# The low part of each freshly transposed y block is computed from PSUM instead of from its copy in SBUF

## The chip, the cores and the metric

The kernel runs on one core of a Trainium2 chip. The metric is the device time of one execution in microseconds (us). The time of a kernel is the median of its runs. One further execution was recorded by the hardware profiler; the durations of single instructions come from that one.

In the profile PE is the matrix engine and PEld its weight load, DVE is the vector engine, ACT the activation engine, POOL the general engine (GpSimd), and SP issues most DMAs. Each engine works through its own queue in order. L1266 is line 1266 of the kernel.

## The reference, cut to what matters

A decoder trunk of two layers runs over a prompt of 2048 tokens (width 1024) and, with the same weights, over eight sample tokens. Everything is float32. Each layer computes

```
u = RMSNorm(x) @ W_in                      # W_in: 1024 x 4880
y = [ mLSTM | Mamba-2 SSD | sliding-window attention ]   # 3 x 512 columns, each with its gate and norm
x = x + concat(y) @ W_out                  # W_out: 1536 x 1024
```

It also returns the state of each of the three mixers. The change touches only the way in which `concat(y)` is brought into `@ W_out`.

## The kernel before, in words

**Precision.** A float32 product is made of three products of a faster format (`F32R`). Each operand is split into a high part, which is the value rounded to that format, and a low part, the value less its high part. The product is then high x high + high x low + low x high.

**Tiling.** The prompt of each layer is cut into four blocks of 512 tokens, so there are eight block passes. A pass runs the input projection by groups of 512 columns, and every group runs over eight chunks of 128 rows of `W_in`. The output projection of a pass (`g == 'out'`) is placed between the groups of the next pass. It has two halves of 512 output columns, and each half runs over twelve chunks `k` of 128 rows of `W_out` (in the last pass the two halves take turns). A chunk is twelve matmuls of 128x128 by 128x512 in `multiply` (L519 with the activations as the moving operand or L521 the other way round): four output tiles, three products each.

**y blocks.** y is kept in SBUF tiles (`yA`, `yB`, `yC`, in the `quad` tiles). Chunks 0 to 3 (mLSTM) and 4 to 7 (SSD) hold tokens on the partitions and must be transposed; chunks 8 to 11 (attention) are already transposed. `prep_y` makes the operands of a chunk, one chunk ahead. When a chunk of k < 8 comes up for the first time (`new`), it

1. transposes the block with four PE instructions (L1252) into `pt`, one of the four PSUM banks of the ring `mx`;
2. lets ACT write the high part `yh` from `pt` (L1259), scaled by the norm weight;
3. lets ACT copy `pt` back over the block in SBUF, `blk` (L1263), where the second half of the projection will find it transposed;
4. puts `low` (L1266, on DVE) into a list of late work. It is emitted in `multiply`, after the second of the four tiles of the chunk before.

`low` computes `yl = blk * weight - yh`. In all there are 192 chunks of y, of which 64 are new (eight in each of the eight passes). For the other 128 there is no transpose and `pt` is `blk` itself.

**Order of the rest.** Mixers, gates and the sample tokens' work are generators ("streams"). `pump` is called after a tile of a chunk and takes a step of a stream if an accounting clock in the program (`Clock`) says that the engines are not too far behind and that the next `mx` bank will be free. The condition on the bank is this line:

```
if st[4] <= now and max(ck.t.values()) <= now + back and ck.free_at(self.rings['mx'][-4]) <= now:
```

`free_at` is the end, by that clock, of the last write or read of the tile that had the bank. The tile framework (`schedule_with_timeline_sim=True`) places semaphores between engines and may change the order further. During the first half of an output projection the streams are mostly the mLSTM of the next pass (`mix_a`, which asks for ten `mx` banks per 128 tokens), the end of the attention of the current pass (`main_c`) and the sample tokens' work.

Of the kernel before, what the change touches and what calls it, by code (L numbers as in the profile page):

```python
# [184 lines left out]
class Build:  # L185
# [1057 lines left out]
    def prep_y(self, ch):  # L1243

        nc, S, k = self.nc, ch['S'], ch['k']
        Y, L = [S['yA'], S['yB'], S['yC']][k // 4], S['L']
        blk = Y[:, :, (k % 4) * 128:(k % 4) * 128 + 128] if k < 8 else Y[:, k % 4, 0:512].rearrange("p (t c) -> p t c", c=128)
        new = ch['new']
        if new:
            pt = self.mx()  # L1250
            for t in range(4):
                nc.tensor.transpose(pt[:, t * 128:t * 128 + 128], blk[:, t, :], self.ident)  # L1252
            pt = pt.rearrange("p (t c) -> p t c", c=128)
        else:
            pt = blk
        i = k % 2

        yh, yl = (self.xTh[i], self.xTl[i]) if S['last'] else self.F[2 * i:2 * i + 2]
        nc.scalar.activation(yh.rearrange("p (t c) -> p t c", c=128), pt, AF.Copy, scale=L['ynw'][:, k:k + 1])  # L1259

        if new:

            nc.scalar.activation(blk, pt, AF.Copy)  # L1263

        def low():
            nc.vector.scalar_tensor_tensor(yl.rearrange("p (t c) -> p t c", c=128), blk, L['ynw'][:, k:k + 1],  # L1266
                                           yh.bitcast(F32).rearrange("p (t c) -> p t c", c=128),
                                           op0=ALU.mult, op1=ALU.subtract)

        self.late.append((0, low))  # L1270
        ch['y'] = (yh, yl)
# [664 lines left out]
```

## Time and profile before

| | |
|---|---|
| runs, us | 2997.62, 3002.35, 2995.71; median 2997.62 |
| profiled execution, us | 2994.12 |
| its span, first to last instruction, us | 2992.3 |
| PE busy | 2903.5 us, 97% of the span |
| DVE busy | 1912.3 us, 64% |
| ACT busy | 1235.0 us, 41% |
| POOL busy | 920.3 us, 31% |
| mean granted clock of PE | 0.991 |

The span leaves out 1.8 us of the profiled execution. A busy share is an average over the whole span. The chain is the work that ended last, followed back from the last instruction to whatever released each step.

### The profile page before, as it was taken

Reading aid. Unit: us, or ns where it says so; the run is one execution under the profiler, and the core shown is the slowest. Engines: PE = TensorE matmul, PEld = TensorE weight load, DVE = VectorE, ACT = ScalarE, POOL = GpSimd, SP = SyncE. Lnnn points to the kernel's source line nnn. Section 1 sums busy time; section 2 is a strip of 40 time slices with the busy share of each in tenths; the row PEclk is TensorE's granted clock in tenths of the full one; section 3 lists DMA queues with packets and bytes.
Section 4 is the critical chain, followed back from the end, with each engine's and each line's share of the span. In section 5 each row is a group of like instructions: output and inputs, shape, how many; then the busy total and the mean of one; then the engine's idle time right before and its main releaser. Section 6 shows DMA issues by size and latency. Waiting matters only on the chain.

```text
span 2992.3 us, 42253 instructions
## 1 busy us (share of the span) xinstructions
PE 2903.5 (97%) x14454; PEld 2373.4 (79%) x14454; DVE 1912.3 (64%) x4323; ACT 1235.0 (41%) x3219; POOL 920.3 (31%) x968
## 2 busy tenths in 40 slices
PE   8999999999999999999999999999999999999988
PEld 7787877788878888888788778887887778788876
DVE  6378567778476763477644686477755677645774
ACT  5343555235432453325544345432444225532344
POOL 5336325244131430116422552332421132200321
PEclk9999999999999999999999999999999999999999
DMA  8755558754575434655556745687545754355533
GB/s 279 241 197 168 174 184 284 248 170 141 164 247 189 151 117 143 199 171 182 184 187 215 240 159 183 205 274 232 161 156 177 244 174 160 131 163 165 177 112 124
DMA packets 245995, 558.82 MB, mean 187 GB/s; under 512 B 49308, under 2 KB 82236, under 8 KB 245732
## 3 DMA queue, kind: packets, MB, share of 16 engines
q1 hardware_dynamic: 245780, 556.12, 57.6%
q8 instruction: 114, 1.87, 0.3%
q14 instruction: 101, 0.83, 0.1%
HBM read 430.46 MB, written 127.87 MB: 187 GB/s over the span
## 4 chain that ended last, share of the span: by engine, by line
PE 71%; DVE 13%; DMA 8%; POOL 3%; ACT 2%; issue 2%; SPq 1%; POOLq 0%; DVEq 0%; ACTq 0%
PE pj L519 29%; PE pj L521 27%; DMA wr<-in_w_in 2%; PE mx L1203 2%; PE mx L1152 2%; PE mx L984 1%; DMA unit<-bcd 1%; DVE quad L659 1%; PE mx L542 1%; PE mx L541 1%; POOL hl L498 1%; ACT unit L1173 1%; PE mx L993 1%; PE mx L1252 1%; DMA unit<-us 1%
## 5 line engine op out<-in xcount | busy, mean ns | idle before, releaser
L521 PE MATMUL pj<-hl,xTh 128*128 128x512 f32 (+1 forms) x3072 | 945.4, 383 | 17.2 <-ACT hl L494 7.6
L519 PE MATMUL pj<-xTh,hl 128*128 128x512 f32 x2240 | 727.5, 402 | 4.8 <-ACT xTh L1259 2.9
L521 PEld LDWEIGHTS pj<-hl,xTh 128*128 128x128 f32 x3072 | 564.6, 189 | 129.0 <-DVE quad L562 8.3
L521 PE MATMUL pj<-hl,xTl 128*128 128x512 f32 (+1 forms) x1536 | 580.4, 381 | 0.0
L519 PE MATMUL pj<-parts,hl 128*128 128x512 f32 x2016 | 518.9, 404 | 15.1 <-DVE parts L1266 8.3
L519 PEld LDWEIGHTS pj<-xTh,hl 128*128 128x128 f32 x2240 | 421.5, 190 | 100.9 <-ACT xTh L1259 3.9
L519 PEld LDWEIGHTS pj<-parts,hl 128*128 128x128 f32 x2016 | 366.9, 189 | 96.1 <-DVE parts L1266 11.2
L519 PE MATMUL pj<-xTl,hl 128*128 128x512 f32 x1120 | 436.0, 398 | 1.9 <-DVE xTl L1266 1.9
L498 POOL TENSOR_TENSOR hl<-wr,hl 128x512 fp32r<-128x512 f32 (+1 forms) x232 | 318.9, 1380 | 356.3 <-ACT hl L494 311.2
L521 PEld LDWEIGHTS pj<-hl,xTl 128*128 128x128 f32 x1536 | 291.1, 189 | 52.5
L1195 POOL TENSOR_TENSOR parts<-parts,cst 128x512 fp32r<-128x512 f32 x120 | 158.6, 1339 | 409.0 <-ACT parts L1188 392.3
L519 PEld LDWEIGHTS pj<-xTl,hl 128*128 128x128 f32 x1120 | 211.2, 189 | 47.7 <-DVE xTl L1266 2.3
L1266 DVE SCALAR_TENSOR_TENSOR parts<-quad,lp,parts 128x512 fp32r<-128x512 f32 x168 | 143.0, 852 | 155.4 <-ACT quad L1263 62.4
L494 ACT ACTIVATE hl<-wr 128x512 fp32r<-128x512 f32 (+1 forms) x232 | 142.2, 615 | 234.2 <-PE mx L542 49.6
L1032 POOL TENSOR_TENSOR unit<-quad,rpqn 128x256 f32<-128x256 f32 x32 | 24.3, 759 | 441.6 <-PE mx L951 166.8
L1173 ACT ACTIVATE unit<-unit,c_m,c_sc 128x128 f32<-128x128 f32 x256 | 123.3, 483 | 69.3 <-DVE c_m L1164 68.8
L1259 ACT ACTIVATE parts<-quad,lp 128x512 fp32r<-128x512 f32 x112 | 80.4, 720 | 155.9 <-PE pj L519 141.1
L659 DVE SCALAR_TENSOR_TENSOR quad<-quad,lp,quad 128x512 f32<-128x512 f32 x192 | 141.8, 781 | 0.3
L1189 DVE TENSOR_TENSOR parts<-mx,parts 128x512 fp32r<-128x512 f32 x64 | 44.0, 687 | 90.2 <-ACT parts L1188 81.0
L384 POOL TENSOR_TENSOR quad<-quad 128x512 f32<-128x512 f32 x24 | 33.5, 1398 | 217.1 <-ACT quad L382 216.4
L1181 ACT ACTIVATE unit<-unit,c_m 128x128 f32<-128x128 f32 x256 | 81.3, 392 | 19.4 <-DVE c_m L1179 19.2
L541 PE MATMUL mx<-hl,samS 128*66 128x512 f32 (+1 forms) x208 | 83.4, 403 | 0.9 <-ACT hl L494 0.9
(409 smaller groups left out, 4551.3 us busy)
## 6 DMA issues: line engine op xcount, KB each, us to landing
hl<-kept SPq DMA_DIRECT2D x552, 512.0 KB
kept<-hl SPq DMA_DIRECT2D x184, 512.0 KB
wr<-in_w_in SPq DMA_DIRECT2D x168, 256.0 KB
hl<-kept SPq DMA_DIRECT2D x48, 272.0 KB
quad<-in_xT SPq DMA_DIRECT2D x40, 256.0 KB
quad<-in_x_prompt SPq DMA_DIRECT2D x16, 512.0 KB
wr<-in_w_out SPq DMA_DIRECT2D x32, 256.0 KB
x<-quad SPq DMA_DIRECT2D x32, 256.0 KB
```

The costliest lines, as they stand in the source:

```text
L494: nc.scalar.activation(h, r, AF.Copy)
L498: nc.gpsimd.tensor_tensor(lw, r, h.bitcast(F32), op=ALU.subtract)
L519: nc.tensor.matmul(ps[t], w[:, tt], a, start=st and first, stop=en and last)
L521: nc.tensor.matmul(ps[t][:, :N], a[:, tt], w[:, :N], start=st and first, stop=en and last)
L541: nc.tensor.matmul(pd[:66, :N], self.samS[:, k, :], hi[:, :N], start=st, stop=False)
L659: nc.vector.scalar_tensor_tensor(acc, u[:, j:j + 512], cw[:, j, c:c + 1], acc, op0=ALU.mult, op1=ALU.add)
L1152: nc.tensor.matmul(o, q, kz[:, a, s, 0:nk, :].rearrange("p n c -> p (n c)"), start=s == 0, stop=s == 1)
L1173: nc.scalar.activation(P(a, j), P(a, j), AF.Exp, bias=nm[:, j:j + 1], scale=head(sc, a, j), accum_out=den[:, j:j + 1])
L1181: nc.scalar.activation(P(a, j), P(a, j), AF.Copy, scale=den[:, j:j + 1])
L1195: nc.gpsimd.tensor_tensor(o.bitcast(F32R), p, self.triu.unsqueeze(1).to_broadcast([128, 4, 128]), op=ALU.mult)
L1259: nc.scalar.activation(yh.rearrange("p (t c) -> p t c", c=128), pt, AF.Copy, scale=L['ynw'][:, k:k + 1])
L1266: nc.vector.scalar_tensor_tensor(yl.rearrange("p (t c) -> p t c", c=128), blk, L['ynw'][:, k:k + 1], yh.bitcast(F32).rearrange("p (t c) -> ...
```

## The change

`low` takes `pt` instead of `blk` as the operand that is scaled. For the 64 new blocks `pt` is the PSUM bank that PE has just filled, and it now has two readers on ACT and one on DVE. For the other 128 blocks `pt` is `blk`, and nothing changes. The ACT copy into `blk` stays.

```diff
         def low():
-            nc.vector.scalar_tensor_tensor(yl.rearrange("p (t c) -> p t c", c=128), blk, L['ynw'][:, k:k + 1],
+            nc.vector.scalar_tensor_tensor(yl.rearrange("p (t c) -> p t c", c=128), pt, L['ynw'][:, k:k + 1],
                                            yh.bitcast(F32).rearrange("p (t c) -> p t c", c=128),
                                            op0=ALU.mult, op1=ALU.subtract)
```

## Rows read from the trace of the kernel before

**Rows 1.** The page: span, and busy time of each engine.
```profile
span 2992.3 us, 42253 instructions
PE 2903.5 (97%) x14454; PEld 2373.4 (79%) x14454; DVE 1912.3 (64%) x4323; ACT 1235.0 (41%) x3219; POOL 920.3 (31%) x968
```

**Rows 2.** Stretches: length, busy PE, PEld, DVE, ACT, POOL; clock; DMA share, GB/s.
```profile
434.00:474.00 40.00, 37.67 (x196) 30.41 (x195) 23.96 (x36) 23.46 (x49) 18.11 (x15) 1.00 0.73 245
...
1544.00:1575.00 31.00, 31.00 (x169) 25.78 (x167) 16.27 (x28) 14.44 (x30) 0.00 (x0) 1.00 0.43 138
...
1946.00:2269.00 323.00, 319.33 (x1603) 263.19 (x1602) 219.40 (x537) 127.94 (x351) 97.34 (x108) 1.00 0.62 202
...
2297.00:2613.00 316.00, 301.81 (x1505) 247.42 (x1503) 210.51 (x491) 117.09 (x332) 75.85 (x89) 1.00 0.57 184
...
2891.00:2934.00 43.00, 41.06 (x212) 34.07 (x213) 30.56 (x61) 25.31 (x62) 9.18 (x8) 1.00 0.41 129
```

**Rows 3.** Line 1266, all instances: durations (ns), then idle time before (us, times).
```profile
L1266 DVE SCALAR_TENSOR_TENSOR parts<-quad,lp,parts x168: 729/752/1871, 438.9 to 2698.3; 128x512 fp32r<-128x512 f32 x168
...
  ACT quad L1263: 68.0, 37
```

**Rows 4.** Line 1263, all instances: durations (ns, least, median, most).
```profile
L1263 ACT ACTIVATE quad<-mx x64: 577/590/641, 437.4 to 2932.9; 128x512 f32<-128x512 f32 x64
```

**Rows 5.** Waits of PE, whole run: us in total, times, longest.
```profile
PE mx L984 <- DVE unit L979: 11.9, 6, 5.4
PE pj L519 <- DVE parts L1266: 8.3, 8, 2.4
PE pj L521 <- ACT hl L494: 7.6, 2, 6.4
...
PE pj L519 <- DVE xTl L1266: 1.9, 1, 1.9
```

**Rows 6.** Waits of PE between 435 and 475 us.
```profile
PE pj L519 <- DVE parts L1266: 0.4, 1, 0.4
```

**Rows 7.** DVE groups by shape: busy us, mean ns, idle before.
```profile
L1189 DVE TENSOR_TENSOR parts<-mx,parts 128x512 fp32r<-128x512 f32 x64 | 44.0, 687 | 90.2 <-ACT parts L1188 81.0 <-POOL hl L498 6.9 <-POOL parts L1195 1.8
...
L562 DVE SCALAR_TENSOR_TENSOR quad<-wP,pj 128x512 f32<-128x512 f32 x64 | 41.4, 680 | 5.5 <-ACT wP L561 5.2
```

**Rows 8.** Line 1119 (ACT): its idle time before, us, times.
```profile
  DVE parts L1120: 54.2, 21
```

**Rows 9.** Timeline around two fresh blocks of the fourth pass: start, duration.
```profile
1547.99 1.03 PE L1252 MATMUL mx<-ident,quad 128*128 128x128 f32 x8
...
1548.68 0.69 ACT L1259 ACTIVATE parts<-mx,lp 128x512 fp32r<-128x512 f32 x1 [0.36 <-PE mx L1252]
...
1549.27 0.59 ACT L1263 ACTIVATE quad<-mx 128x512 f32<-128x512 f32 x1
...
1550.67 0.75 DVE L1266 SCALAR_TENSOR_TENSOR parts<-quad,lp,parts 128x512 fp32r<-128x512 f32 x1
```

**Rows 10.** Timeline at the first fresh blocks of the last pass.
```profile
2892.54 0.59 ACT L1263 ACTIVATE quad<-mx 128x512 f32<-128x512 f32 x1
...
2893.99 3.26 DVE L915 TENSOR_SCALAR quad<-quad,rq_y 128x256 f32<-128x256 f32 x8
...
2895.19 0.60 PE L1252 MATMUL mx<-ident,quad 128*128 128x128 f32 x4
...
2897.17 1.40 DVE L1266 SCALAR_TENSOR_TENSOR xTl<-quad,lp,xTh 128x512 fp32r<-128x512 f32 x2
2897.96 0.77 PEld L519 LDWEIGHTS pj<-xTl,hl 128*128 128x128 f32 x4 [2.25 <-DVE xTl L1266]
```

**Rows 11.** Chain that ended last: its pieces on line 1266 among fresh blocks.
```profile
438.95 0.66 DVE parts L1266
...
445.16 0.67 DVE parts L1266
...
2897.25 0.67 DVE xTl L1266
```

## The prediction

> **What bounds the kernel now.** I read the page first. PE is busy for 2903.5 of 2992.3 us [rows 1], so all its idle time is 88.8 us, and a change can gain only what it takes out of that or out of PE's own work. The change alters no PE instruction. The next question is therefore where those 88.8 us lie, and for that I cut the span into the eight stretches in which fresh y blocks are made and what lies between them. The reader is to see that PE is busy for the whole of six of the eight, as in the fourth (31.00 of 31.00 us), and idle for 40.00 - 37.67 = 2.3 us in the first and 43.00 - 41.06 = 1.9 us in the last [rows 2]. Together 4.3 us of idle PE stand where the change acts. Third, I read line 1266 itself. DVE sat idle before it for 68.0 us, 37 times, until the ACT copy on line 1263 was done [rows 3]. This is the wait that the change can shorten. Fourth, I asked whether PE waits for the result. In the whole run it waited 8.3 + 1.9 us for line 1266 [rows 5]; of this 0.4 us falls into the first stretch [rows 6], and the 1.9 us are those of the last stretch. The rest, 7.9 us, falls on old blocks, which the change leaves alone. So DVE waits for the copy, and hardly anything waits for DVE.
>
> **The change part by part.**
>
> *The wait that goes.* Today low needs the high part and then the copy. The copy takes 0.590 us (median, 64 times) [rows 4], and it is the last to end. If low needs only the high part, each of the 37 waits can shrink by up to that: 37 x 0.59 = 21.8 us of idle DVE, at most. What is late next is the operand's other reader, the high part on ACT, and behind it DVE's queue. On PE's path this is worth nothing while PE has other tiles to work on: the cover is the chunk before, whose remaining products run while low is made. In the fourth pass the copy ended at 1549.27 + 0.59 = 1549.86 us and low began at 1550.67 us, 0.81 us later, because DVE was in its queue's earlier work [rows 9]. There the copy isn't the last to end at all. If the cover were gone everywhere, the price of the wait would be what PE waits in the two stretches that are not full, 0.4 + 1.9 = 2.3 us. The 1.9 us come from DVE's queue too: the copy ended at 2892.54 + 0.59 = 2893.13 us, the eight instructions on line 915 ran to 2897.25 us, and low followed [rows 10]. So I take 0 and keep a gain of 2.3 us as the bound.
>
> *The operand that moves to PSUM.* No instruction of before has just this form. The nearest are 128x512 float32 on DVE with one operand in PSUM and one in SBUF: 687 ns (line 1189, also a low part) and 680 ns (line 562, also a scalar-tensor-tensor) [rows 7]. Line 1266 with both operands in SBUF has a median of 752 ns, and up to 1871 ns [rows 3]. I take 752 - 684 = 68 ns less for each of the 64: 64 x 0.068 = 4.4 us of DVE work. The bounds are 0 (PSUM costs what SBUF costs) and 64 x 0.072 = 4.6 us. On the path this counts where the chain runs through fresh low parts, which is three pieces of 0.66 to 0.67 us [rows 11]: 3 x 0.07 = 0.2 us.
>
> [...]
>
> *The bank that is held longer.* This is the wait that the change adds. PE's next write into the bank must wait until DVE's low is done, where today it waits for ACT's copy. Behind that write on PE stand the projection's matmuls (L519), the very work that fills PE. In the fourth pass the bank would be held until 1550.67 + 0.75 = 1551.42 us instead of 1549.86 us: 1.56 us more [rows 9]. In the last pass it would be held to 2897.17 + 0.70 = 2897.87 us instead of 2893.13 us: 4.7 us more [rows 10]. The ring has four banks, so the fourth request after the fresh block is the one that can meet this. PE's own wait there isn't in the trace. Below it is 0, when the bank comes round after low is done. Above it is the whole time held, and 64 x 1.56 us would be 100 us, far from what the full stretches allow. `pump` asks the program's clock for the bank before it takes a step and puts the step off otherwise, so the wait should turn into steps taken a tile later while the matmuls run on. I take 0 for the path and price the rest as a rival.
>
> *The order of the work.* The copy stays, and no DMA is issued, moved or removed. But two schedulers read the change: `Clock` sees low depend on an earlier instruction and the bank come free later, and the framework sees low ready earlier. From about 437 us on, where the first fresh copy starts [rows 4], the order of steps can differ. The trace can't show the new order. How much an order is worth I bound from the eight stretches between the fresh ones (the last runs to the end). They hold much the same kind of work, and PE is idle in them for between 323.00 - 319.33 = 3.7 us and 316.00 - 301.81 = 14.2 us [rows 2]. Half of that distance, 5 us, taken as the change of one stretch with its sign open, gives over eight of them 5 x sqrt(8), some 14 us either way. Most of the distance comes from work that differs between layers and passes, so I keep about two thirds of it, 9 to 10 us, as what a new order usually reaches.
>
> *The sum*, against the profiled execution: 2994.1 (its own time; span 2992.3 and 1.8 us around it) - 0 for the wait - 0.2 for the shorter instruction + 0 for the bank = 2993.9 us. The median of the runs is 3.5 us above the profiled execution, so this is 2997.4 us as a median. I forecast 2997 us, no change that can be told. Runs of before lie between 2995.71 and 3002.35 us, and about 0.2% (6 us) is what a measurement of this kernel can tell from no change.
>
> **The rivals.**
>
> *A. Low still waits for the copy.* In the trace an ACT instruction that reads a bank (line 1119, second half) sat idle for 54.2 us, 21 times, until DVE's read of the same bank on line 1120 was done [rows 8]. The two also write into one tile, so the row doesn't tell which of these makes it wait. If readers of a bank are kept one behind the other, low would wait for the copy as before, and the change does nothing but shorten 64 instructions: 2994.1 - 0.2 us, 2997.4 us as a median. Against it stands that no row shows two readers of one bank without another tie between them. [...]
>
> *B. Faster: DVE comes earlier and the order falls well.* The pieces are the 2.3 us of PE's waits on fresh low parts [rows 5, 6], and a DVE that is up to 21.8 us of waiting and 4.4 us of work lighter. Where PE waits for DVE elsewhere, it can gain: line 984 waited 11.9 us for line 979 in six times, and 8.3 us fell on line 1266 [rows 5]. Half of these two, 10 us, with 2 us of the direct ones, gives 2994 - 12, about 2985 us as a median. Against it: those waits lie outside the eight stretches, and six of the eight have no idle PE to give back.
>
> *C. Slower: the held bank puts off the streams.* The place is the request for the fourth `mx` bank after a fresh block. The price of one put-off step is a tile, three matmuls; in the full fourth stretch PE did 169 instructions in 31.00 us, 0.18 us each [rows 2], so a tile is some 0.6 us, and it costs nothing while PE is full. It becomes dear when the stream arrives late at the point where the program drains it, for then PE waits for a chain of other engines, as it does now for line 979: 11.9 us / 6 = 2.0 us a time, 5.4 us at most [rows 5]. It decides from three such waits on (6 us). With one in each of seven passes it is 14 us, 3011 us; with five, 3007 us. For it speaks that in the last pass two fresh banks would be held for 4.7 us while PE already transposes the next block at 2895.19 us [rows 10]. Against it speaks that a bank held for 1.56 us more is seldom the one that comes next in a ring of four.
>
> **How the numbers follow.** No change that can be told gets 0.50. In 0.20 of this rival A holds, in 0.30 low starts earlier and nothing on PE's path notices. B gets 0.21 and C 0.29: B needs idle PE that is not there in the stretches concerned, C needs only a bank that comes round early, and both share the new order. Within 0.2% lies 2991 to 3003 us, so that this band alone is the likeliest case's own range. To leave out 2 in 10 the range reaches past it on both sides, to 2985 us (B as priced) and to 3010 us (C with six late streams). Faster by over 0.2%: 0.21; within 0.2%: 0.50; slower by over 0.2%: 0.29.
>
> **What would show each step.** [...] The wait: idle time of DVE before the fresh low parts ends by line 1259 (the high part) and no longer by line 1263, and 68.0 us shrink to about 46 us or less; if line 1263 is still named, A holds. The bank: PE's waits name line 1266 from instructions that write `mx` (transposes and mixers) and no longer from L519 alone. The order: in the stretches of fresh blocks PE stays full; in those between them its idle time moves by a few us in either direction. The prediction is wrong if PE's idle time of 88.8 us moves by over 6 us, and I expect the fault then in the order of the steps, not in low itself.

## The result, and the profile after

The changed kernel is slower: 3013.64 us (median of 4 runs, 3011.36 to 3019.07) against 2996.66 us (4 runs, 2994.95 to 3002.35). The ratio is 1.0069, 95% interval 1.0053 to 1.0085; the two medians alone lie 17.0 us or 0.57% apart. The forecast was 2997 us with a range up to 3010 us.

The page of the changed kernel, span and busy time of each engine, beside [rows 1]:

```profile
span 3009.6 us, 42229 instructions
...
PE 2915.3 (97%) x14454; PEld 2381.3 (79%) x14454; DVE 1915.3 (64%) x4323; ACT 1232.7 (41%) x3219; POOL 921.5 (31%) x968
```

PE did the same 14454 instructions, but was busy 2915.3 - 2903.5 = 11.8 us longer and idle 94.3 - 88.8 = 5.5 us longer; together that is the 17.3 us by which the span grew. Most of the busy part, 9.7 of the 11.8 us, was lost to the lower clock, 0.50 of the full one. The mean clock fell from 0.991 to 0.987, which is (1 - 0.987) x 3009.6 - (1 - 0.991) x 2992.3 = 12.2 us more of full-speed time that was not granted, idle time included. Counted in the two traces only where PE was busy, the time lost to the lower clock is 30.5 against 20.8 us, 9.7 us more. (The mean clock by itself does not tell a run's time: runs of the kernel before with a mean of 0.988 took 2990.18 to 3001.27 us.) PE stood still longer, and behind some of the stops the granted clock was 0.50; one such stretch, 752 to 756 us, is shown below.

Line 1266 of the changed kernel, all instances: durations in ns (least, median, most), then DVE's idle time before it. It answers [rows 3].

```profile
L1266 DVE SCALAR_TENSOR_TENSOR parts<-quad,lp,parts x112: 732/752/1782, 470.9 to 2716.7; 128x512 fp32r<-128x512 f32 x112
L1266 DVE SCALAR_TENSOR_TENSOR parts<-mx,lp,parts x56: 732/751/753, 441.4 to 2661.0; 128x512 fp32r<-128x512 f32 x56
...
  ACT quad L1263: 70.5, 41
```

The change is there (`mx` stands where `quad` stood), but neither of its two promised gains is. The fresh low parts take 751 ns, no less than the old ones. And DVE still waits for the ACT copy on line 1263: 70.5 us in 41 times, against 68.0 us in 37. Two rows of the timeline show one such wait, first the copy on ACT, then low on DVE:

```profile
1560.45 0.59 ACT L1263 ACTIVATE quad<-mx 128x512 f32<-128x512 f32 x1
...
1561.07 0.75 DVE L1266 SCALAR_TENSOR_TENSOR parts<-mx,lp,parts 128x512 fp32r<-128x512 f32 x1 [4.97 <-ACT quad L1263]
```

The copy ended at 1561.04 us and low began 0.03 us later, though it no longer reads what the copy writes. Both read one PSUM bank, and the tile framework keeps them one behind the other. That no other tie does this is shown by the experiment below in which the copy stands behind low: there the copy waits for low.

PE's waits in the changed kernel (us in total, times, longest), beside [rows 5]:

```profile
PE mx L984 <- DVE unit L979: 12.5, 5, 5.6
PE pj L519 <- DVE parts L1266: 8.6, 6, 3.9
PE pj L521 <- ACT quad L622: 8.1, 2, 5.2
...
PE pj L519 <- DVE xTl L1266: 0.9, 1, 0.9
```

Waits on line 1266 hardly moved (9.5 us against 10.2). So the time was not lost at low. To find the place, I read the stretches of fresh blocks again. Columns as in [rows 2]; the first stretch, the one between it and the second, then the fourth:

```profile
436.00:476.00 40.00, 37.90 (x192) 30.01 (x191) 20.53 (x33) 22.67 (x48) 17.07 (x14) 1.00 0.69 236
476.00:808.00 332.00, 322.92 (x1595) 265.23 (x1594) 229.09 (x539) 137.00 (x376) 118.70 (x121) 0.98 0.61 198
...
1558.00:1586.00 28.00, 28.00 (x150) 23.11 (x150) 14.45 (x24) 11.91 (x23) 0.00 (x0) 1.00 0.43 145
```

The stretches of fresh blocks stay as full as they were. The place shows in the first transposes (line 1252) of the first and of the second stretch, here of the kernel before and then of the changed one:

```profile
434.57 0.60 PE L1252 MATMUL mx<-ident,quad 128*128 128x128 f32 x4
...
793.39 0.49 PE L1252 MATMUL mx<-ident,quad 128*128 128x128 f32 x3
...
437.07 0.60 PE L1252 MATMUL mx<-ident,quad 128*128 128x128 f32 x4
...
808.62 0.49 PE L1252 MATMUL mx<-ident,quad 128*128 128x128 f32 x3
```

From one to the other it is 808.62 - 437.07 = 371.6 us, and in the kernel before 793.39 - 434.57 = 358.8 us. So 12.7 us are lost there, nearly all in work that the change does not touch. (The 14 us named in an expectation below are the same distance read in steps of 2 us.) The first 2.5 us, by which the first transpose itself is late, are scatter between two executions, for up to there the order of the two programs is the same. In steps of 20 us the largest loss stands at the end of the distance. The kernel before:

```profile
730.00:750.00 20.00, 20.00 (x99) 16.40 (x98) 17.66 (x71) 10.73 (x32) 4.25 (x4) 1.00 0.62 208
750.00:770.00 20.00, 20.00 (x99) 16.45 (x98) 5.30 (x11) 8.58 (x24) 5.08 (x4) 1.00 0.61 200
```

and the changed one:

```profile
730.00:750.00 20.00, 18.11 (x93) 13.82 (x91) 19.64 (x48) 9.91 (x29) 10.57 (x14) 1.00 0.51 168
750.00:770.00 20.00, 17.87 (x72) 14.67 (x73) 13.36 (x61) 11.97 (x39) 0.55 (x1) 0.83 0.40 129
```

The clock in the second of these, in a finer step:

```profile
752.00:756.00 4.00, 3.87 (x12) 3.15 (x13) 3.13 (x20) 3.93 (x10) 0.00 (x0) 0.50 0.16 65
```

DVE (third busy figure) is full in the changed kernel, PE stands still for 1.9 + 2.1 us, and then the clock is at its lower level for a while, 0.50 from 752 to 756 us and 0.83 in the mean of the step. PE does 72 instructions in the last step where it did 99. With 17.87 x 0.17 = 3.0 us for the clock, these two steps hold some 7 of the 12.7 us; the rest lies in smaller pieces. What filled DVE there is the question for the experiments.

### The profile page after: what moved, and what is told of

It is laid out like the page before. It is cut to its first block, busy times and chain, and to the rows that moved or that the text cites. A ratio compares the mean times of both kernels' runs of the same rounds, so it can differ in the third digit from the quotient of the medians.

```text
span 3009.6 us, 42229 instructions
## 1 busy us (share of the span) xinstructions
PE 2915.3 (97%) x14454; PEld 2381.3 (79%) x14454; DVE 1915.3 (64%) x4323; ACT 1232.7 (41%) x3219; POOL 921.5 (31%) x968
## 4 chain that ended last, share of the span: by engine, by line
PE 76%; DVE 12%; DMA 6%; POOL 2%; ACT 2%; issue 2%; SPq 0%; POOLq 0%; DVEq 0%; ACTq 0%
PE pj L519 32%; PE pj L521 28%; PE mx L1203 2%; PE mx L1152 2%; PE mx L984 1%; PE mx L542 1%; PE mx L541 1%; DVE quad L443 1%; PE mx L857 1%; PE mx L850 1%; PE mx L1252 1%; DMA quad<-x 1%; PE mx L1186 1%; DMA unit<-bcd 1%; PE mx L993 1%
## 5 line engine op out<-in xcount | busy, mean ns | idle before, releaser
L1266 DVE SCALAR_TENSOR_TENSOR parts<-quad,lp,parts 128x512 fp32r<-128x512 f32 x112 | 95.8, 859 | 97.0 <-PE pj L519 66.0
L653 ACT ACTIVATE quad<-quad 128x512 f32<-128x512 f32 x64 | 40.5, 632 | 135.1 <-DVE quad L659 134.6
L815 ACT ACTIVATE unit<-quad 128x128 f32<-128x128 f32 x128 | 39.6, 309 | 132.0 <-DVE quad L873 129.4
```

## The experiments

The program can be told one thing and do another: `Clock`, the account by which `pump` decides when a stream takes its next step, can be shown another operand than the one that low reads. That separates the order from the instruction.

**The changed low, and the account sees the copy.** `told` puts `blk` in the place of `pt` in the account, for the fresh blocks alone.

```diff
-            ins = [x for x in i.ins if hasattr(x, 'bass_ap')]
+            ins = [self.swap.get(x.bass_ap.tensor.name, x) for x in i.ins if hasattr(x, 'bass_ap')]
...
         def low():
-            nc.vector.scalar_tensor_tensor(yl.rearrange("p (t c) -> p t c", c=128), blk, ...
+            self.told(pt, blk, new); nc.vector.scalar_tensor_tensor(yl.rearrange("p (t c) -> p t c", c=128), pt, ...
```

> The changed low (it reads the PSUM bank), but the program's accounting clock is told that it reads the copy in SBUF, so that the steps of the streams are emitted in the order of the kernel before; what remains of a different order on PE (1193 lines of difference against 5292) comes from the tile framework. Theory 'order': the time is lost through the order that the accounting clock sets, so this kernel is within 5 us of before, about 2997 us. Theory 'instruction': the time is lost on the chip, by the bank that is held or the operand that is read, so this kernel is as slow as the changed one, about 3013 us. Theory 'framework': the loss comes from the framework's own reordering, which is still there: 3005 us or more.

Measured: 3000.7 us against 2995.38 us, ratio 1.0016 (1.0006 to 1.0026). Most of the 0.69% is gone, though low reads PSUM. What is left is 5.3 us, at the edge of what 'order' had allowed.

**The low of before, and the account sees the bank.** The complement: `self.told(blk, pt, new)`, with `blk` as the operand.

> The low part of before (it reads the copy), but the accounting clock is told that it reads the PSUM bank, so that the steps are emitted in the order of the changed kernel. Theory 'order': as slow as the changed kernel, 3009 to 3018 us, although no instruction differs from before except in its place. Theory 'instruction': as fast as before, about 2997 us.

Measured: 3007.35 us against 2995.38 us, ratio 1.0041 (1.0029 to 1.0053). No instruction differs from before except in its place, and more than half of the loss is back. It is less than 'order' had expected (3009 us or more), and 0.41% is less than the changed kernel's 0.69%; with the 0.16% of the first kernel it comes near it.

**The account sees the bank in the first stretch alone, and in all but the first.** Both have the changed low; the edit is the condition.

```diff
-            self.told(pt, blk, new); nc.vector.scalar_tensor_tensor(yl...
+            self.told(pt, blk, new and S['n'] > 0); nc.vector.scalar_tensor_tensor(yl...
```

(`S['n'] == 0` for the complement.)

> The changed low everywhere; the accounting clock sees the bank read by low in the first of the eight stretches of fresh blocks alone (the output projection of pass 0) and the copy in the other seven. Between the landmarks of the first and the second stretch the changed kernel lost 14 of its 17 us. Theory 'order, put-off steps of one pass': nearly all of the loss is here, 3008 to 3014 us. Theory 'order, a little in every pass': about 2 us of the loss, 2999 us. Theory 'instruction': 3013 us.

> The complement of the kernel that treats the first stretch alone: the accounting clock sees the copy in the first stretch of fresh blocks and the bank in the other seven. Theory 'order, put-off steps of one pass': about 3 us over before, 3000 us. Theory 'order, a little in every pass': 3010 us or more. Theory 'instruction': 3013 us.

Measured against 2995.38 us: the first stretch alone 3011.44 us, 1.0055 (1.0034 to 1.0077); all but the first 3001.95 us, 1.0021 (1.0011 to 1.0031). Both as 'put-off steps of one pass' had it. Against the kernel whose account sees the copy everywhere (3000.7 us), the first stretch is worth some 11 us and the seven others 1 us.

How many steps are put off there, the program itself can say. Printed while it emitted the instructions, the calls of `pump` in which a stream was held up by a fresh bank alone were these (stream, time of the account in ns, how long the bank would be held):

```
d 459673 held 1499      sample tokens' work, step that starts dec_a
d 460328 held 844       the same step
d 460983 held 189       the same step
a 460983 held 189       mix_a
```

In the first stretch one step of the sample stream is put off by three tiles and one step of the mLSTM by one tile; in the whole program there are six more such calls. Put off in the kernel whose account sees the copy, the mLSTM's step alone changes no row of the order of PE and DVE, and the sample stream's alone gives the order of 'the first stretch alone' but for a few rows. So what separates these two kernels is one step, 2 us late by the account. Their traces show what became of it. The sample stream's transposes on line 1431, on line 1700 at its end, and the norm on line 915 (durations in ns, first and last start), and the two steps of 20 us; first with the copy in the account:

```profile
L1431 PE MATMUL mx<-ident,unit x4: 201/202/222, 466.2 to 466.4; 8*128 8x8 f32 x4
...
L1700 PEld LDWEIGHTS mx<-ident,unit x4: 84/87/87, 607.4 to 607.8; 128*8 128x8 f32 x4
...
L915 DVE TENSOR_SCALAR quad<-quad,rq_y x8: 348/350/1134, 729.8 to 731.6; 128x256 f32<-128x256 f32 x8
...
730.00:750.00 20.00, 20.00 (x97) 16.54 (x96) 14.33 (x67) 11.89 (x38) 1.16 (x1) 1.00 0.50 171
```

then with the bank in the account, in the first stretch alone; the last row is a wait of PE between 735 and 765 us:

```profile
L1431 PE MATMUL mx<-ident,unit x4: 202/212/223, 468.3 to 470.2; 8*128 8x8 f32 x4
...
L1700 PEld LDWEIGHTS mx<-ident,unit x4: 84/85/89, 620.1 to 620.5; 128*8 128x8 f32 x4
...
L915 DVE TENSOR_SCALAR quad<-quad,rq_y x8: 341/346/1364, 743.9 to 747.4; 128x256 f32<-128x256 f32 x8
...
730.00:750.00 20.00, 16.41 (x76) 12.09 (x76) 18.94 (x47) 10.61 (x31) 9.02 (x8) 1.00 0.64 215
750.00:770.00 20.00, 20.00 (x89) 16.57 (x90) 11.23 (x57) 11.05 (x38) 2.49 (x2) 0.91 0.42 121
...
PE mx L1152 <- DVE parts L1120: 2.7, 2, 2.0
```

The sample stream is 2.1 us late on line 1431 and 12.7 us late at its last transposes. DVE work that had been done by 733 us now reaches to 748 us: the SSD's norm ends 16 us later, ahead of the attention's line 1120 in DVE's queue. PE waits for that and for others, 3.6 us in this step, and the clock is 0.91 in the next.

The delay has no fixed price. Four of the six further calls are the same four again, with the same waits, in the fifth stretch, the first of the second layer. The sample stream falls back there by as much. First the kernel whose account sees the copy, then 'all but the first':

```profile
L1431 PE MATMUL mx<-ident,unit x4: 201/202/223, 1939.1 to 1939.3; 8*128 8x8 f32 x4
...
L1700 PEld LDWEIGHTS mx<-ident,unit x4: 84/87/87, 2080.4 to 2080.8; 128*8 128x8 f32 x4
...
L1431 PE MATMUL mx<-ident,unit x4: 202/212/223, 1951.0 to 1952.9; 8*128 8x8 f32 x4
...
L1700 PEld LDWEIGHTS mx<-ident,unit x4: 84/85/89, 2103.3 to 2103.8; 128*8 128x8 f32 x4
```

From line 1431 to line 1700 it takes 152.3 instead of 141.3 us, as it takes 151.8 instead of 141.2 us in the first stretch. Yet the seven stretches together cost 1 us by the medians. In the two profiled executions the distance from the fifth first transpose to the sixth is 358.8 instead of 352.6 us, and the next one is 343.2 instead of 346.0 us, so part of it comes back. The late stream as such is therefore not the price. What its work meets later has to be, and that was followed in the first stretch alone.

**Orders that have no reason to be worse.** Is it this bank, or would any other order do? In the kernel before one constant of the account was changed, `HOP = 250.0` to 260, 240 and 249 ns.

> The kernel before with one constant of the accounting clock changed: the delay between engines is taken as 260 instead of 250 ns. No instruction differs except in its place (3932 lines of difference in PE's order). It measures how far the time moves with an order that has no reason to be better or worse. Theory 'any other order': the order of before is a good draw and most others are slower by 0.2 to 0.7%, so 3001 to 3016 us. Theory 'this bank': a neutral change of order moves the time by less than 0.2% either way, and the loss needs the steps that the held bank puts off.

> The same with 240 ns; 8615 lines of difference in PE's order, more than the change itself makes (5292). Theory 'any other order': 3001 to 3016 us. Theory 'this bank': within 0.2% of before.

> The same with 249 ns, a small step: 1469 lines of difference in PE's order, about as many as remain in the kernel whose clock is told that low reads the copy (1193), which was 0.16% slower than before. Theory 'any other order': 0.1 to 0.3% slower, as that one. Theory 'this bank': no difference, and the 0.16% then come from the instruction.

Measured against 2995.58 us: 260 ns 3010.02 us, 1.0041 (1.0027 to 1.0055); 240 ns 3014.35 us, 1.0057 (1.0040 to 1.0074); 249 ns 2997.27 us, 1.0003 (0.9994 to 1.0012). The two that moved much of the order cost about what the change cost, as 'any other order' had expected; the small step of 249 ns cost nothing that shows, as 'this bank' had expected. The two lose the time elsewhere. The kernel with 240 ns loses the most between the first transposes of the third and the fourth stretch, 397.5 against 387.0 us. Between 730 and 770 us PE is full in both, as in this row of the kernel with 240 ns:

```profile
730.00:750.00 20.00, 20.00 (x108) 17.07 (x107) 17.41 (x74) 7.87 (x20) 6.98 (x6) 1.00 0.59 194
```

Its page shows the same two shares of the loss, idle and busy time of PE (100.9 and 2914.4 us):

```profile
span 3015.3 us, 42266 instructions
...
PE 2914.4 (97%) x14454; PEld 2382.1 (79%) x14454; DVE 1926.9 (64%) x4323; ACT 1235.6 (41%) x3219; POOL 918.2 (30%) x968
```

**The copy behind low.** With the changed low, the ACT copy is emitted after it instead of before it.

```diff
-        if new:
-
-            nc.scalar.activation(blk, pt, AF.Copy)
...
-                                           op0=ALU.mult, op1=ALU.subtract)
+                                           op0=ALU.mult, op1=ALU.subtract); new and nc.scalar.activation(blk, pt, AF.Copy)
```

> The changed low, and the ACT copy into SBUF is emitted behind it instead of ahead of it. In the changed kernel low still waits for that copy; here low needs only the high part, and the copy waits for low. The idle time of DVE before fresh low parts that ends with line 1263 goes to nothing and is named by line 1259 instead. Theory 'the wait was worth nothing': the time does not get better for it; what the kernel shows is again its order, 2997 to 3015 us. Theory 'the wait is the loss' (low and copy one behind the other are what costs): back to 2997 us or under.

Measured: 3014.39 us against 2995.58 us, ratio 1.0059 (1.0044 to 1.0074). DVE's idle time before line 1266, and who waited for line 1266 (the copy now stands on line 1268):

```profile
  ACT parts L1259: 94.1, 49
...
  ACT quad L1268: 37.2, 40
```

The wait for the copy is gone, as asked, and the copy waits for low in its place. PE gained nothing by it. The kernel has an order of its own, so a gain of a few us could hide in it; a large one could not.

**The instruction alone.** With the framework's timeline scheduling off, in both kernels, the engines follow the order of emission. The pair is the low of before and the changed low with the account told of the copy; 85 of 11332 rows of PE's order differ.

```diff
-    with tile.TileContext(nc, schedule_with_timeline_sim=True) as tc, ExitStack() as ctx:
+    with tile.TileContext(nc, schedule_with_timeline_sim=False) as tc, ExitStack() as ctx:
```

> The kernel before with the framework's timeline scheduling switched off, so that the engines work in the order in which the program emits the instructions. It is the base for the kernel beside it. Expected by every theory: slower than before, since PE now stops at each wait of a stream; 3020 to 3150 us.

> The changed low (it reads the PSUM bank), the accounting clock told that it reads the copy, and the framework's timeline scheduling off: of all 11332 rows of PE's order 85 lines differ from the kernel beside it, so that nearly nothing but the instruction and the held bank is left. Theory 'order': within 0.1% of that kernel. Theory 'instruction': the 0.16% that the kernel with the clock told of the copy lost against before are here again, 4 to 6 us slower than the one beside it; if the whole 0.7% were the instruction, 20 us slower.

Measured: 3124.05 us (3122.59 to 3125.87) with the low of before, 3119.44 us (3116.55 to 3123.56) with the changed one. The instruction and the bank that it holds cost nothing that shows; the changed low is 4.6 us, 0.15%, ahead, with ranges that overlap. That is a little outside the 0.1% of 'order', and the other way round from 'instruction'.

**The scalar operand.** In the changed low `L['ynw'][:, k:k + 1]` is replaced by `0.5`, so the kernel leaves the norm weights out of the low part. It was run once; its use is in the durations.

> The changed low with the constant 0.5 where the norm weight (one value per partition) stood, in all 192 low parts: the weights are left out of the low part. It asks why the fresh low takes 751 ns and not the 684 ns of the rows that the sum was made from, both of which have no per-partition scalar. Theory 'the scalar operand costs it': the 64 fresh ones drop to 675 to 695 ns, and the 128 others, with both tensors in SBUF, drop by about as much, to 680 to 700 ns in the median. Theory 'PSUM costs it': the fresh ones stay at 740 to 755 ns.

Line 1266 in that kernel, the fresh blocks last:

```profile
L1266 DVE SCALAR_TENSOR_TENSOR parts<-quad,parts x112: 669/693/1775, 465.9 to 2716.3; 128x512 fp32r<-128x512 f32 x112
L1266 DVE SCALAR_TENSOR_TENSOR parts<-mx,parts x56: 672/692/693, 436.3 to 2660.6; 128x512 fp32r<-128x512 f32 x56
```

Both fall by 59 ns in the median, from 751 or 752 ns. The scalar costs it, not the place of the tensor. The single run took 3011.87 us (before: 2993.68 us), as slow as the changed kernel.

## Why the prediction was wrong, point by point

**The wait that goes: right in worth, wrong in fact.** It was costed at nothing for PE, and nothing speaks against that: where the copy was moved behind low and the wait did go, nothing was gained. But it did not go in the change itself. (The low part at 1550.67 us [rows 9], by which the copy is not the last to end, was an exception: of the nine in that stretch, six waited for the copy.) Rival A's mechanism (readers of a bank one behind the other) is what the framework does: low waits for the copy (70.5 us, 41 times), and with the copy behind it the copy waits for low (37.2 us, 40 times). A was right about the wait and wrong about the time, because it left the order out.

**The operand in PSUM: mis-sized.** The term was 64 x 0.068 = 4.4 us of DVE; in the median it measured 752 - 751 ns, nothing. The rows chosen as nearest [rows 7] lacked the per-partition scalar, which is worth 59 ns. By its place alone the operand is neither cheaper nor dearer in the median: 751 against 752 ns with the scalar, 692 against 693 ns without it.

**The bank that is held longer: the step that failed, with the order of the work.** The prediction took 0 for this on the path, and for C it asked for three or more put-off steps that reach a drain late, 2.0 us each. The place was right: `pump` asks for the fresh bank and holds a step back. Given the bank in low's place and the copy's dependency as well, the account emits the changed kernel's order to the row on PE, DVE and ACT, so it is the bank alone that alters that order, and not the earlier start. The price was wrong, and with it the step of the prediction by which a put-off step costs nothing while the matmuls run on. One step of the sample stream, put off by 2 us, ends as some 11 us in the first stretch alone, not because it is waited for, but because every later decision of `pump` and of the framework falls out differently and DVE's work bunches up 270 us further on.

**The order of the work: the right cause, taken as 0 in the sum.** "9 to 10 us either way" lies among what new orders cost (the neutral ones: 1.7, 14 and 19 us by their medians), and is about half of the 17.0 us that came. That it would be a loss was not foreseen. Three neutral orders, none of them faster, suggest that the order of before is a favourable one, which a new order more easily loses than betters; three draws do not prove it. (The six kernels with the low part, the copy or the account changed are slower too, by 5 to 19 us, but theirs are not neutral draws.) Taken so, rival C's case, or simply "another order", should have had more than half of the chance.

**Where a loss can show: one place left out.** The prediction counted only PE's idle time, 88.8 us, and would be wrong if it moved by over 6 us. It moved by 5.5 us. Two thirds of the growth, 11.8 us, came as busy time, 9.7 us of it lost to the lower clock, and the sum had no term for that.

**What stays open.** The kernel whose account sees the copy is 0.16% slower than before. The pair without the timeline scheduling speaks against the instruction, so what is left is the framework's own reordering (1193 rows of PE's order); this is by exclusion, not shown. The kernel with 249 ns speaks the other way: 1469 rows differ there and nothing is lost. Nor was it followed in the neutral orders which step they lose by.

## What to carry to other kernels

Where a program decides its order from an account of its own, each operand is also an entry in that account. Before costing an edit, ask which of the account's conditions reads the buffer that the edit holds longer or frees sooner; here what mattered most was that `pump` asks for the bank. Then measure a few orders that differ for no reason: their scatter (here up to 0.6%) is what a small edit has to beat, and telling the account the old story while the code does the new thing separates the two.

## What the runs showed of the hardware that was not expected

A low part whose two tensors lie in SBUF has the same median as one with a tensor in PSUM (752 and 751 ns), but not the same spread. In the changed kernel the 112 of the first kind reach 1782 ns and their mean is 859 ns; the 56 of the second kind end at 753 ns with a mean of 749 ns:

```profile
L1266 DVE SCALAR_TENSOR_TENSOR parts<-quad,lp,parts 128x512 fp32r<-128x512 f32 x112 | 95.8, 859 | 97.0 <-PE pj L519 66.0 <-ACT parts L1259 27.7 <-PE mx L392 2.0
...
L1266 DVE SCALAR_TENSOR_TENSOR parts<-mx,lp,parts 128x512 fp32r<-128x512 f32 x56 | 41.9, 749 | 67.8 <-ACT quad L1263 67.3 <-issue 0.4
```

The trace also shows what stretches the first kind. A GpSimd (POOL) instruction and a low part of each kind, in order of time:

```profile
463.40 1.29 POOL L498 TENSOR_TENSOR hl<-wr,hl 128x512 fp32r<-128x512 f32 x1 [2.83 <-ACT hl L494]
464.42 0.75 DVE L1266 SCALAR_TENSOR_TENSOR parts<-mx,lp,parts 128x512 fp32r<-128x512 f32 x1 [0.42 <-ACT quad L1263]
...
489.93 1.29 POOL L498 TENSOR_TENSOR hl<-wr,hl 128x512 fp32r<-128x512 f32 x1
490.02 1.75 DVE L1266 SCALAR_TENSOR_TENSOR parts<-quad,lp,parts 128x512 fp32r<-128x512 f32 x1
```

Of all 128 low parts of the changed kernel with both tensors in SBUF, 20 began over 0.2 us before the end of a GpSimd instruction that was already running. Each of these 20 ended 546 to 554 ns after that instruction did, and they are all that took longer than 760 ns. Of the 64 with a tensor in PSUM, 11 began in the same way and took 750 to 752 ns. So the move to PSUM does take low out of the way of GpSimd. For the 64 fresh blocks that is little: their low parts take 47.9 us together, and in the kernel before 49.3 us (taken there in the order of line 1259), four of which took over 800 ns.
